# A trunk block on one core: sixteen column blocks of the input projection summed by chunks, and retention moved into the blocks behind them

## The chip, the cores and the metric

The kernel runs on one core of a Trainium2 chip. The metric is the device time of one launch in microseconds (us); the lower, the better. A core has TensorE (PE in the profile; it multiplies matrices and writes PSUM), VectorE (DVE), ScalarE (ACT), GpSimd (POOL) and SyncE (SP, which issues most of the DMAs here). Each engine works through its own list of instructions, and semaphores make it wait for the others.

## The reference, cut to what matters

One layer of a decoder trunk, 256 tokens of 2048 features, all in float32:

```python
mod = silu(c) @ w_ada + b_ada                       # sh1, sc1, g1, sh2, sc2, g2: 2048 each
xn = rmsnorm(h, norm1_g) * (1 + sc1) + sh1
proj = xn @ w_in                                    # 2048 x 18432
q, k, v, g_ret, bg, cg, xc, gate_logits = split(proj)   # 2048 each, gate_logits 4096
q, k = rotary(q, positions), rotary(k, positions)   # 8 heads of 256
y_ret = (norm(retention(q, k, v)) * silu(g_ret)) @ w_ret_o
y_conv = (bg * causal_conv3(cg * xc)) @ w_conv_o
gate_a, gate_b = split(sigmoid(gate_logits + b_gate))
h = h + g1 * ((gate_a * y_ret + gate_b * y_conv) @ w_mix_o)
xn2 = rmsnorm(h, norm2_g) * (1 + sc2) + sh2
h = h + g2 * ((silu(causal_conv3(xn2 @ w_gate) + b) * (xn2 @ w_up)) @ w_down)
out = rmsnorm(h, final_g)
```

## The kernel before

Every weight passes through the core once, as **units** of 256 rows by 512 columns (512 KB). A unit is loaded on SP's queue into one of six `raw` buffers, then prepared: ACT rounds it to a 12-bit `hi` (line 300, `hi<-raw`), DVE takes the rest as `lo` (line 301, `lo<-raw,hi`). PE then multiplies hi by hi, hi by lo and lo by hi, and adds them in PSUM. `hi` and `lo` have three buffers each; in the first stage every third unit lies in a spare buffer of a pool named `big` instead (`hl`).

There are three ways to multiply a unit. `x_block` and `start_block` hold the tokens still and stream the weights: 12 matmuls of 512 columns (lines 372 to 374). `w_block` holds the weights still: 8 matmuls of 512 columns and 8 of 256 (lines 406 and 410). `start_turned` holds the weights still too, with 24 matmuls of 256 columns (lines 517 to 519), so that four tiles of 256 columns fit into two PSUM banks.

The whole program is one list of units, and small calls between them. `w_ada` goes another way: an `Ada` entry is 512 KB that DVE multiplies by a column of silu(c) and adds up (line 337); it has no matmul until its column sums are taken (line 351).

In the first stage xn is not yet known as a whole, since sh1 and sc1 come out of `w_ada`. So it is made in five chunks of its 2048 features (256, 512, 512, 512, 256). After a chunk, the rows of `w_in` which it frees are multiplied for ten column blocks: four of v, four of the swish gate (`sg`), one of q, one of k. The Ada entries of the next chunk are spread between those units by `spread`. A block's sum over a chunk waits in SBUF: ACT copies it out for the first chunk (lines 462 and 523), DVE adds it for each later one (lines 465 and 525), two instructions a block. One gate block keeps its sum in PSUM. Then follow the six other blocks of q and k as `rot_block` (a `w_block`), and behind each pair of them the retention of two heads: DVE turns q and k by the rotary angles (`rotate`, lines 626 to 629), PE makes the scores (653, 656), DVE multiplies them by the decay (660, 661), PE multiplies by v (672 to 674), ACT sums squares (228), POOL takes the root (222), DVE multiplies by that and by the gate (683), PE turns the result (699), and ACT and DVE split it (92, 93). `after(n, f)` puts such a step n entries later. Then come the merge gates and `w_ret_o`, the conv branch (`conv_blocks`, four times three `w_block`s), `w_conv_o`, `w_mix_o` and the feed-forward half, which the change leaves alone.

The loop at the end walks the list: it loads nine entries ahead and prepares four ahead in the first stage, two later. The tile framework then fixes the order on each engine; it goes by this program order, by when buffers come free and by its own estimates.

## Time and profile before

| | |
|---|---|
| median of 3 runs | 1928.77 us (1926.56 to 1931.59) |
| span of the profiled execution | 1927.2 us |
| busy: PE, DVE, ACT, POOL | 1879.1, 1367.4, 904.8, 22.3 us |
| DMA | 450.88 MB, 234 GB/s over the span |
| chain that ended last | PE 92%, DVE 3%, DMA 2% |

The span runs from the first to the last instruction of the profiled execution; no other time of that execution is given, and its span is 1.6 us under the median of the runs. The busy time of matmuls is modelled and overlaps from one to the next, so a PE that is busy all through a stretch has no gap in it, but how fast it goes is read from how many matmuls stand in the stretch.

### The profile page before, as it was taken

What the parts mean: (1) busy time and instruction counts of PE and PEld (TensorE: products, weight loads), DVE (VectorE), ACT (ScalarE), POOL (GpSimd) and SP (SyncE); (2) the same over time, 40 slices, a digit from 0 to 9 for tenths busy, and PEclk for the clock granted to TensorE, in tenths of its full rate; (3) what the DMA queues carried; (4) which work ended last, traced back from release to release, by engine and by line L of the source; (5) the groups of instructions that cost most, each with busy time, mean ns of one, the idle gap of its engine ahead of it and who ended that gap; (6) DMA issues with size and microseconds to landing.
All of it is one profiled execution on the core that took longest, in us unless ns stands there. A gap on an engine that the chain in (4) does not pass through costs nothing.

```text
span 1927.2 us, 26558 instructions
## 1 busy us (share of the span) xinstructions
PE 1879.1 (98%) x10151; PEld 1615.0 (84%) x10151; DVE 1367.4 (71%) x1690; ACT 904.8 (47%) x1187; POOL 22.3 (1%) x52
## 2 busy tenths in 40 slices
PE   5999999999999999999999999999999999999998
PEld 4788888888888888888888787888888888888886
DVE  6889987776766778767777786666665556666655
ACT  3544444444444444444444445555554335555543
POOL 1000000000000000000000000000000000000000
PEclk8899999999999999999999999999999999999999
DMA  8989866666888888787888895666666666666663
GB/s 300 322 305 335 294 217 188 192 201 213 266 266 259 271 263 265 256 279 251 269 270 295 302 321 153 192 186 186 196 189 193 195 190 188 186 188 186 211 192 126
DMA packets 220288, 450.88 MB, mean 234 GB/s; under 512 B 14516, under 2 KB 23040, under 8 KB 219648
## 3 DMA queue, kind: packets, MB, share of 16 engines
q1 hardware_dynamic: 218784, 445.84, 72.4%
q10 hardware_dynamic: 864, 3.15, 0.4%
q8 instruction: 79, 1.29, 0.3%
q14 instruction: 49, 0.40, 0.1%
q0 software_dynamic: 512, 0.20, 0.0%
HBM read 447.03 MB, written 2.10 MB: 233 GB/s over the span
## 4 chain that ended last, share of the span: by engine, by line
PE 92%; DVE 3%; DMA 2%; issue 1%; ACT 1%; POOL 0%; SPq 0%; POOLq 0%; DVEq 0%; ACTq 0%
PE acc L406 41%; PE acc L410 21%; PE acc L373 8%; PE acc L374 8%; PE acc L372 8%; DMA raw<-in_w_ada 2%; DVE lo L301 1%; PE misc L351 1%; PE acc L519 1%; PE acc L517 1%; PE acc L518 1%; DVE ada L337 0%; PE misc L247 0%; PE misc L653 0%; ACT hi L300 0%
## 5 line engine op out<-in xcount | busy, mean ns | idle before, releaser
L406 PE MATMUL acc<-xn,hi 128*128 128x512 f32 x3072 | 1078.6, 396 | 4.5 <-DVE sb L766 2.1
L300 ACT CAST hi<-raw 128x1024 fp32r<-128x1024 f32 x616 | 648.1, 1052 | 845.9 <-PE acc L406 546.6
L301 DVE TENSOR_TENSOR lo<-raw,hi 128x1024 fp32r<-128x1024 f32 x616 | 749.9, 1223 | 361.7 <-ACT hi L300 360.5
L410 PE MATMUL acc<-xn,lo 128*128 128x256 f32 x3072 | 859.8, 280 | 0.0
L406 PEld LDWEIGHTS acc<-xn,hi 128*128 128x128 f32 x3072 | 576.6, 188 | 140.7 <-DVE sb L766 2.4
L410 PEld LDWEIGHTS acc<-xn,lo 128*128 128x128 f32 x3072 | 580.4, 189 | 1.0 <-issue 0.5
L337 DVE SCALAR_TENSOR_TENSOR ada<-raw,c_act,ada 128x1024 f32<-128x1024 f32 (+1 forms) x199 | 239.4, 1203 | 127.2 <-DMA raw<-in_w_ada 126.1
L373 PE MATMUL acc<-lo,ff_t 128*128 128x512 f32 x332 | 129.2, 389 | 0.0
L374 PE MATMUL acc<-hi,ff_t 128*128 128x512 f32 x332 | 129.2, 389 | 0.0
L372 PE MATMUL acc<-hi,ff_t 128*128 128x512 f32 x332 | 129.2, 389 | 0.0
L416 ACT COPY sb<-acc 128x256 f32<-128x256 f32 x224 | 82.3, 367 | 37.9 <-PE acc L410 30.7
L406 PE MATMUL acc<-conv_t,hi 128*128 128x512 f32 x256 | 90.6, 399 | 0.0
L406 PE MATMUL acc<-y_t,hi 128*128 128x512 f32 x256 | 90.2, 396 | 0.0
L410 PE MATMUL acc<-y_t,lo 128*128 128x256 f32 x256 | 72.2, 282 | 1.7 <-DVE lo L301 1.4
L372 PEld LDWEIGHTS acc<-hi,ff_t 128*128 128x128 f32 x332 | 62.3, 188 | 13.1
L374 PEld LDWEIGHTS acc<-hi,ff_t 128*128 128x128 f32 x332 | 62.3, 188 | 13.0
L373 PEld LDWEIGHTS acc<-lo,ff_t 128*128 128x128 f32 x332 | 62.3, 188 | 12.6
L410 PE MATMUL acc<-conv_t,lo 128*128 128x256 f32 x256 | 71.9, 281 | 0.0
L373 PE MATMUL acc<-lo,xn 128*128 128x512 f32 x172 | 69.1, 402 | 1.8 <-DVE lo L301 1.8
L372 PE MATMUL acc<-hi,xn 128*128 128x512 f32 x172 | 68.2, 404 | 1.6 <-ACT hi L300 1.6
L374 PE MATMUL acc<-hi,xn 128*128 128x512 f32 x172 | 68.7, 399 | 0.0
L406 PEld LDWEIGHTS acc<-conv_t,hi 128*128 128x128 f32 x256 | 48.1, 188 | 12.1
(204 smaller groups left out, 1638.2 us busy)
## 6 DMA issues: line engine op xcount, KB each, us to landing
raw<-in_w_in SPq DMA_DIRECT2D x288, 512.0 KB, 4.8
raw<-in_w_ada SPq DMA_DIRECT2D x176, 512.0 KB, 4.6
raw<-in_w_gate SPq DMA_DIRECT2D x88, 512.0 KB, 4.4
raw<-in_w_up SPq DMA_DIRECT2D x88, 512.0 KB, 4.3
raw<-in_w_down SPq DMA_DIRECT2D x88, 512.0 KB, 4.3
raw<-in_w_ret_o SPq DMA_DIRECT2D x32, 512.0 KB, 4.7
raw<-in_w_conv_o SPq DMA_DIRECT2D x32, 512.0 KB, 5.4
raw<-in_w_mix_o SPq DMA_DIRECT2D x32, 512.0 KB, 5.9
```

What stands on the lines that cost most here:

```text
L300: nc.scalar.copy(self.hi, self.raw)
L301: nc.vector.tensor_tensor(self.lo, self.raw, self.hi.bitcast(F32), op=ALU.subtract)
L337: nc.vector.scalar_tensor_tensor(acc, self.raw[:, k], c_act[:, kt:kt + 1], acc, op0=ALU.mult, op1=ALU.add)
L351: nc.tensor.matmul(ps[:, i:i + 1], lhsT=flat[:, (s0 + i) * P:(s0 + i + 1) * P], rhs=ones[:, 0:1], start=True, stop=True,)
L372: nc.tensor.matmul(ps, lhsT=xh, rhs=u.hi[:, k, :], start=k0 + k == first, stop=False)
L373: nc.tensor.matmul(ps, lhsT=xh, rhs=u.lo[:, k, :], start=False, stop=False)
L374: nc.tensor.matmul(ps, lhsT=xl, rhs=u.hi[:, k, :], start=False, stop=k0 + k == end - 1)
L406: nc.tensor.matmul(ps, lhsT=u.hi[:, k, i * P:(i + 1) * P], rhs=xk.rearrange("p h s -> p (h s)"), start=first, stop=False,)
L410: nc.tensor.matmul(ps[:, 0:S], lhsT=u.lo[:, k, i * P:(i + 1) * P], rhs=xk[:, 0, :], start=False, stop=last,)
L416: nc.scalar.copy(b, ps[:, S:2 * S])
L517: nc.tensor.matmul(ps, lhsT=wh, rhs=xk[:, 0, :], start=first, stop=False)
L518: nc.tensor.matmul(ps, lhsT=wh, rhs=xk[:, 1, :], start=False, stop=False)
```

## The change

Sixteen blocks are summed by chunks where ten were: all four blocks of q and of k now go through `start_turned`, in the order v, sg, q, k for each pair of heads. The sums of q and k lie in the pool `big` (the `hl` buffers are gone from it). `rot_block` is gone. The retention of a pair begins (`begin`: both rotations, then the gate's swish) at fixed places in a list made of the last chunk and of the first conv blocks, which moved ahead of the merge gates. All entries are prepared two ahead. `rotate` works in place with one buffer fewer.

```diff
-PREP_START = 4
-TAILS = (0, 6, 3, 4, 6)
+TAILS = (0, 3, 4, 4, 6)
-IN_BIG = (1, 3)
-ROT_AT = 24
-DEFER_SG, DEFER_ROT = (6, 14, 30, 44), 4
+PAIR_AT, PAIR_STEP = 8, 9
-ADA_QK, ADA_RET, ADA_CONV, ADA_OUT = 8, 28, 42, 32
+ADA_LAST, ADA_CONV0, ADA_RET, ADA_CONV, ADA_OUT = 8, 10, 30, 36, 30
...
-                after(DEFER_SG[j - 4], lambda: swish(d))
+                swishes[j - 4].append(lambda: swish(d))
...
-                if k0 + UK == KT:
-                    after(DEFER_ROT, lambda: done(st["sum"]))
...
-    blocks = [start_block(j, j in IN_PSUM) for j in range(8)]
-    ret0 = {}
-    for key in "qk":
-        col = 0 if key == "q" else D
-        blocks.append(start_turned(col, (lambda key: lambda x: rotate(x, ret0, key))(key)))
+    blocks = []
+    for pair in range(4):
+        blocks += [start_block(j, j in IN_PSUM) for j in (pair, 4 + pair)]
+        blocks += [start_turned(i * D + pair * CB, sums_of(pair, i)) for i in range(2)]
...
-        t1 = w4("rot", [P, 4, S])
         o = w4("rotated", [P, 4, S])
-        nc.vector.tensor_tensor(t1, xx, wide(cos_t, 4), op=ALU.mult)
+        nc.vector.tensor_tensor(o, xx, wide(cos_t, 4), op=ALU.mult)
         nc.vector.tensor_tensor(xx, xx, wide(sin_t, 4), op=ALU.mult)
-        nc.vector.tensor_tensor(o[:, 0::2, :], t1[:, 0::2, :], xx[:, 1::2, :], op=ALU.subtract)
-        nc.vector.tensor_tensor(o[:, 1::2, :], t1[:, 1::2, :], xx[:, 0::2, :], op=ALU.add)
+        nc.vector.tensor_tensor(o[:, 0::2, :], o[:, 0::2, :], xx[:, 1::2, :], op=ALU.subtract)
+        nc.vector.tensor_tensor(o[:, 1::2, :], o[:, 1::2, :], xx[:, 0::2, :], op=ALU.add)
...
+        def begin():
+            rotate(qk_sums[pair][:, 0], st, "q")
+            rotate(qk_sums[pair][:, 1], st, "k")
+            for f in swishes[pair]:
+                f()
+            after(3, scores)
...
+    seq = spread(last_chunk, take(ada_mid, ADA_LAST)) + spread(conv_blocks(0), take(ada_mid, ADA_CONV0))
+    for pair in range(4):
+        seq.insert(PAIR_AT + PAIR_STEP * pair, Call(retention(pair)))
+    seq.insert(2, Call(load_decay))
+    units += seq
...
-        ahead = PREP_START if i < n_start else PREP_AHEAD
-        while prepped <= min(i + ahead, n - 1):
+        while prepped <= min(i + PREP_AHEAD, n - 1):
```

Below, the units of the first chunk are called Z0, Z1, ..., those of the last chunk L0 to L15 (v, sg, q, k of pair 0, then of pair 1, and so on), and those of the first conv blocks C0 to C23. So L4 to L7 are v, sg, q and k of pair 1.

First place, the list of DVE where the rotation of pair 0 stands. Before, the eight instructions of the two rotations stand between `lo`s:

```order
L626 TENSOR_TENSOR rot_2452<-sum_565,cos_t 128x1024
L525 TENSOR_TENSOR sum_597<-acc_2370,sum_597 128x512
L525 TENSOR_TENSOR sum_597<-acc_2371,sum_597 128x512
L301 TENSOR_TENSOR lo_2427<-raw_2246,hi_2426 128x1024
L627 TENSOR_TENSOR sum_565<-sum_565,sin_t 128x1024
L337 SCALAR_TENSOR_TENSOR ada_2202<-raw_2367,c_act,ada_2202 128x1024
L301 TENSOR_TENSOR lo_2433<-raw_2268,hi_2432 128x1024
L628 TENSOR_TENSOR rotated_2453<-rot_2452,sum_565 128x2x256
L629 TENSOR_TENSOR rotated_2453<-rot_2452,sum_565 128x2x256
L301 TENSOR_TENSOR lo_2461<-raw_2290,hi_2460 128x1024
L626 TENSOR_TENSOR rot_2480<-sum_597,cos_t 128x1024
```

In the changed kernel the same place reads as follows; `lo_3680` is the `lo` of L6, `acc_3658` the second half of the sum of L4, `acc_3696` and `acc_3697` that of L5, and `lo_3715` the `lo` of L7:

```order
L298 TENSOR_TENSOR lo_3680<-raw_3557,hi_3679 128x1024
L462 TENSOR_TENSOR v_tok_227<-acc_3658,v_tok_227 128x512
L625 TENSOR_TENSOR rotated_3683<-qk_371,cos_t 128x1024
L625 TENSOR_TENSOR rotated_3688<-qk_371,cos_t 128x1024
L626 TENSOR_TENSOR qk_371<-qk_371,sin_t 128x1024 x2
L627 TENSOR_TENSOR rotated_3683<-rotated_3683,qk_371 128x2x256
L628 TENSOR_TENSOR rotated_3683<-rotated_3683,qk_371 128x2x256
L627 TENSOR_TENSOR rotated_3688<-rotated_3688,qk_371 128x2x256
L628 TENSOR_TENSOR rotated_3688<-rotated_3688,qk_371 128x2x256
L462 TENSOR_TENSOR sg_tok_228<-acc_3696,sg_tok_228 128x512
L462 TENSOR_TENSOR sg_tok_229<-acc_3697,sg_tok_229 128x512
L298 TENSOR_TENSOR lo_3715<-raw_3584,hi_3714 128x1024
```

Both rotations now stand in one piece, with no `lo` between the one of L6 and the one of L7.

Second place, the list of DVE where pair 2 begins, behind C0 (whose `lo` is `lo_4100`; the two adds of L15, `qk_767<-acc_4103` and its other half, and the first split `y_t_4131<-misc_4132` stand between that and these rows). Before, such steps of retention had `lo`s between them, as for the second pair:

```order
L301 TENSOR_TENSOR lo_2668<-raw_2458,hi_2667 128x1024
L626 TENSOR_TENSOR rot_2653<-qk_2630,cos_t 128x1024
L301 TENSOR_TENSOR lo_2709<-raw_2486,hi_2708 128x1024
L627 TENSOR_TENSOR qk_2630<-qk_2630,sin_t 128x1024
L93 TENSOR_TENSOR y_t_2691<-misc_2692,y_t_2691 128x2x256
L628 TENSOR_TENSOR rotated_2654<-rot_2653,qk_2630 128x2x256
L629 TENSOR_TENSOR rotated_2654<-rot_2653,qk_2630 128x2x256
L93 TENSOR_TENSOR y_t_2691<-misc_2699,y_t_2691 128x2x256
L301 TENSOR_TENSOR lo_2731<-raw_2508,hi_2730 128x1024
```

And now, up to `lo_4166`, the `lo` of C1:

```order
L90 TENSOR_TENSOR y_t_4131<-misc_4139,y_t_4131 128x2x256
L334 SCALAR_TENSOR_TENSOR ada_3347<-raw_3942,c_act,ada_3347 128x1024
L625 TENSOR_TENSOR rotated_4147<-qk_625,cos_t 128x1024
L625 TENSOR_TENSOR rotated_4152<-qk_625,cos_t 128x1024
L626 TENSOR_TENSOR qk_625<-qk_625,sin_t 128x1024 x2
L627 TENSOR_TENSOR rotated_4147<-rotated_4147,qk_625 128x2x256
L628 TENSOR_TENSOR rotated_4147<-rotated_4147,qk_625 128x2x256
L627 TENSOR_TENSOR rotated_4152<-rotated_4152,qk_625 128x2x256
L628 TENSOR_TENSOR rotated_4152<-rotated_4152,qk_625 128x2x256
L477 TENSOR_TENSOR sg_tok_228<-sg_tok_228,sig_4157 128x512
L477 TENSOR_TENSOR sg_tok_229<-sg_tok_229,sig_4160 128x512
L298 TENSOR_TENSOR lo_4166<-raw_3973,hi_4165 128x1024
```

Fifteen instructions, those of a split, an Ada step, two rotations and the swish among them, now stand between the `lo` of C0 and that of C1. For pair 1 ten stand between those of L11 and L12, for pair 3 ten between those of C6 and C7.

Third place, the list of ACT in the first chunk. Before, the first units are all of v, and the copies of one (line 462) stand ahead of the next `hi`:

```order
L300 CAST hi_334<-raw_299 128x1024
L462 COPY v_tok_227<-acc_317 128x512
L462 COPY v_tok_226<-acc_350 128x512
L462 COPY v_tok_227<-acc_351 128x512
L300 CAST hi_368<-raw_332 128x1024
L462 COPY v_tok_226<-acc_384 128x512
L462 COPY v_tok_227<-acc_385 128x512
L300 CAST hl_402<-raw_366 128x1024
```

In the changed kernel `hi_403` belongs to Z4 and `hi_459` to Z5; `acc_369` is a sum of Z2, `acc_407` and `acc_408` those of Z3, `acc_441` and `acc_442` those of Z4:

```order
L297 CAST hi_342<-raw_283 128x1024
L297 CAST hi_365<-raw_303 128x1024
L520 COPY qk_371<-acc_369 128x512
L520 COPY qk_371<-acc_370 128x512
L297 CAST hi_403<-raw_312 128x1024
L520 COPY qk_371<-acc_407 128x512
L520 COPY qk_371<-acc_408 128x512
L459 COPY v_tok_226<-acc_441 128x512
L459 COPY v_tok_227<-acc_442 128x512
L297 CAST hi_459<-raw_340 128x1024
L297 CAST hi_468<-raw_363 128x1024
```

So the `hi` of Z5 stands behind copies of the very unit ahead of it, Z4; the same holds for Z9, behind copies of Z8. From Z4 on, the `hi`s of the other units stand behind copies of the unit two ahead, or of none; that of Z14 also has the six instructions ahead of it that make xn of the second chunk.

## Rows read from the trace of the kernel before

**Rows 1.** The page: busy time, and the span in 40 equal slices.
```profile
PE 1879.1 (98%) x10151; PEld 1615.0 (84%) x10151; DVE 1367.4 (71%) x1690; ACT 904.8 (47%) x1187; POOL 22.3 (1%) x52
...
PE   5999999999999999999999999999999999999998
...
DVE  6889987776766778767777786666665556666655
...
PEclk8899999999999999999999999999999999999999
```

**Rows 2.** Windows by stage: stretch, length, each engine's busy us (instructions), granted clock, DMA.
```profile
32.68:70.26 37.58, 29.44 (x91) 20.47 (x92) 31.70 (x33) 17.06 (x24) 0.00 (x0) 0.71 0.90 308
70.26:97.80 27.54, 27.54 (x145) 23.77 (x144) 22.19 (x22) 13.86 (x18) 0.00 (x0) 1.00 0.95 321
97.80:280.12 182.32, 181.68 (x977) 157.41 (x976) 167.61 (x212) 80.17 (x89) 0.00 (x0) 1.00 0.87 293
280.12:460.00 179.88, 179.48 (x1031) 157.02 (x1030) 134.82 (x172) 78.59 (x121) 4.05 (x4) 1.00 0.63 193
460.00:480.00 20.00, 18.78 (x106) 15.90 (x105) 11.46 (x13) 9.37 (x15) 0.00 (x0) 1.00 0.66 217
```

**Rows 3.** Windows: 13 units of 512-column matmuls, 4 of `start_turned`, 7 of `w_block`.
```profile
143.84:179.20 35.36, 35.36 (x157) 29.28 (x156) 35.36 (x37) 11.63 (x12) 0.00 (x0) 1.00 1.00 357
126.82:138.34 11.52, 11.52 (x98) 11.52 (x96) 9.51 (x13) 7.97 (x11) 0.00 (x0) 1.00 0.72 223
317.56:336.97 19.41, 19.41 (x114) 16.98 (x113) 13.76 (x15) 8.66 (x11) 0.00 (x0) 1.00 0.68 217
```

**Rows 4.** Groups of DVE by form: count | busy us, mean ns | idle before.
```profile
L301 DVE TENSOR_TENSOR lo<-raw,hi 128x1024 fp32r<-128x1024 f32 x616 | 749.9, 1223 | 361.7 <-ACT hi L300 360.5
L337 DVE SCALAR_TENSOR_TENSOR ada<-raw,c_act,ada 128x1024 f32<-128x1024 f32 x169 | 217.0, 1284 | 126.9 <-DMA raw<-in_w_ada 126.1
L465 DVE TENSOR_TENSOR v_tok<-acc,v_tok 128x512 f32<-128x512 f32 x32 | 21.4, 686 | 1.6 <-PE acc L374 1.4
L626 DVE TENSOR_TENSOR rot<-qk,cos_t 128x1024 f32<-128x1024 f32 x6 | 7.3, 1224 | 0.1
L628 DVE TENSOR_TENSOR rotated<-rot,qk 128x512 f32<-128x512 f32 x6 | 4.1, 688 | 0.1
L660 DVE TENSOR_TENSOR pt<-misc,decay 128x256 f32<-128x256 f32 x8 | 3.4, 420 | 0.6 <-PE misc L656 0.6
L661 DVE TENSOR_TENSOR pt<-misc,decay 128x128 f32<-128x128 f32 x8 | 2.3, 282 | 0.0
L683 DVE SCALAR_TENSOR_TENSOR y_tok<-misc,r_y,sg_tok 128x256 f32<-128x256 f32 x16 | 6.6, 478 | 4.7 <-POOL r_y L222 4.7
L93 DVE TENSOR_TENSOR y_t<-misc,y_t 128x512 fp32r<-128x512 f32 x8 | 5.2, 683 | 0.0
```

**Rows 5.** Chain that ended last, retention of pair 0: start us, us, what.
```profile
294.42 0.86 PE misc L653 x4
...
296.59 0.44 PE misc L656 x4
...
302.59 0.43 PE misc L672 x2
...
304.75 0.45 PE misc L674 x2
...
311.30 0.87 PE misc L699 x8
```

**Rows 6.** Timeline of the first chunk: start us, us, engine, instruction [idle before <-releaser].
```profile
42.96 0.59 ACT L462 COPY v_tok<-acc 128x512 f32<-128x512 f32 x1 [0.54 <-PE acc L374]
43.44 1.05 ACT L300 CAST hi<-raw 128x1024 fp32r<-128x1024 f32 x1
44.54 0.73 PE L372 MATMUL acc<-hi,xn 128*128 128x512 f32 x2 [1.62 <-ACT hi L300]
...
46.46 0.50 PE L373 MATMUL acc<-lo,xn 128*128 128x512 f32 x1 [1.18 <-DVE lo L301]
```

More of the change, by code (lines that the diff above doesn't have):

```diff
@@ L496, in start_block, with start_turned @@
                 for n, ch in enumerate(chunks)]
-    def start_turned(col, done):
+    def start_turned(col, sums):
         st = {}
@@ L507, in run @@
                 if k0 == 0:
-                    st["sum"] = w4("sum", [P, 4, S])
+                    st["sum"] = sums()
                 for i in range(4):
@@ L531, in start_turned, with sums_of, sums @@
                 for n, ch in enumerate(chunks)]
-    blocks = [start_block(j, j in IN_PSUM) for j in range(8)]
-    ret0 = {}
-    for key in "qk":
-        col = 0 if key == "q" else D
-        blocks.append(start_turned(col, (lambda key: lambda x: rotate(x, ret0, key))(key)))
+    qk_sums = {}
+    swishes = [[] for _ in range(4)]
+    def sums_of(pair, i):
+        def sums():
+            if pair not in qk_sums:
+                qk_sums[pair] = blk8("qk", [P, 2, 4, S], F32)
+            return qk_sums[pair][:, i]
+        return sums
+    blocks = []
+    for pair in range(4):
+        blocks += [start_block(j, j in IN_PSUM) for j in (pair, 4 + pair)]
+        blocks += [start_turned(i * D + pair * CB, sums_of(pair, i)) for i in range(2)]
     def spread(seq, extra, tail=0):
@@ L556, in tile_trunk_block @@
         seq = [u for b in blocks for u in b[n]]
-    units += seq
-    for i, u in enumerate([u for u in units if isinstance(u, Weights)]):
-        u.in_big = i % IN_BIG[1] < IN_BIG[0]
     units.insert(40, Call(turn_vectors))
     units.insert(5, Call(prep=lambda: turned(*vec1)))
-    units.insert(len(units) - ROT_AT, Call(rest_of_rotary))
-    units.insert(len(units) - ROT_AT + 6, Call(sines))
-    n_start = len(units) - 12
+    units.insert(len(units) - 10, Call(rest_of_rotary))
+    units.insert(len(units) - 4, Call(sines))
+    last_chunk = seq
     g1b = {}
@@ L703, in turn @@
                 split(ps.rearrange("p (k s) -> p k s", k=2), yb[:, 2 * g:2 * g + 2])
-        st["next"] = scores
-        return st
+        def begin():
[4 more added lines that the diff above has]
+            after(3, scores)
+        return begin
     def load_decay():
@@ L710, in load_decay @@
         tc.keep_in_program_order(nc.scalar.dma_start(dec["t"], decay))
-    units.insert(len(units) - 8, Call(load_decay))
-    seq = []
-    for pair in range(4):
-        st = retention(pair, ret0 if pair == 0 else {})
-        if pair > 0:
-            seq += rot_block(pair * CB, st, "q")
-            seq += rot_block(D + pair * CB, st, "k")
-    units += spread(seq, take(ada_mid, ADA_QK))
     def gate_block(col, store, key):
@@ L730, in gate_block @@
         return in_block(col, e)
-    mixp = {}
-    def ret_block(j, store):
-        def e(i, a, b):
-            if j % 2 == 0 and i == 0:
-                mixp[j // 2] = blk8("mixp", [P, 8, S], F32)
-            nc.vector.tensor_tensor(b, a, b, op=ALU.add)
-            nc.vector.tensor_tensor(
-                mixp[j // 2][:, (4 * j + i) % 8, :], b, store["g"][:, i, :], op=ALU.mult
-            )
-        return w_block(w_ret_o, j * CB, lambda kt: y_t[kt // 4][:, kt % 4], e)
-    seq = []
-    for j in range(4):
-        st = {}
-        seq += gate_block(7 * D + j * CB, st, "g")
-        seq += ret_block(j, st)
-    units += spread(seq, take(ada_mid, ADA_RET))
     conv_t = []
@@ L786, in conv_blocks, with ret_block, e @@
                 + in_block(4 * D + j * CB, e_b))
+    seq = spread(last_chunk, take(ada_mid, ADA_LAST)) + spread(conv_blocks(0), take(ada_mid, ADA_CONV0))
[3 more added lines that the diff above has]
+    units += seq
+    mixp = {}
+    def ret_block(j, store):
+        def e(i, a, b):
+            if j % 2 == 0 and i == 0:
+                mixp[j // 2] = blk8("mixp", [P, 8, S], F32)
+            nc.vector.tensor_tensor(b, a, b, op=ALU.add)
+            nc.vector.tensor_tensor(
+                mixp[j // 2][:, (4 * j + i) % 8, :], b, store["g"][:, i, :], op=ALU.mult
+            )
+        return w_block(w_ret_o, j * CB, lambda kt: y_t[kt // 4][:, kt % 4], e)
     seq = []
     for j in range(4):
+        st = {}
+        seq += gate_block(7 * D + j * CB, st, "g")
+        seq += ret_block(j, st)
+    units += spread(seq, take(ada_mid, ADA_RET))
+    seq = []
+    for j in range(1, 4):
         seq += conv_blocks(j)
```

14 lines of the change are left out of this document (2 added, 12 removed).

## The prediction

> **What bounds the kernel now.** I read the page first, then windows by stage, then one window for each kind of unit, then the groups of DVE, and last the chain and the timeline where a term needs them. The page shows PE busy 98% and DVE 71% [rows 1]; the 40 slices show that this share of DVE is an average over first slices with digits of 8 and 9 and a rest with 5 to 7. The windows say where PE is not busy. From 32.68 to 70.26 us it has 29.44 busy us of 37.58, at a mean granted clock of 0.71 (between the two levels, 1.2 and 2.4 GHz); from there to 460 us it lacks 1.0 us in 390 in all [rows 2]. So PE's work sets the time; what a change can win ahead of 460 us lies in the first chunk, and whatever keeps PE waiting later is added in full.
>
> PE does a unit in 35.36 / 13 = 2.72 us with 512-column matmuls, 11.52 / 4 = 2.88 us in `start_turned`, and 19.41 / 7 = 2.77 us in `w_block` [rows 3]. In the first chunk it did six units in 37.58 us, where 6 x 2.72 = 16.3 would do: 21.3 us are lost there.
>
> DVE was busy 167.61 of 182.32 us from 97.80 on, without making PE wait [rows 2]: a DVE that is 92% busy isn't yet the bound. What matters is how many units stand prepared when a long piece of DVE work comes.
>
> **The change, part by part.**
>
> *Kind of unit.* Six blocks of eight units go from `w_block` to `start_turned`: 48 x (2.88 - 2.77) = +5.3 us on PE. The rows show both kinds at full clock and without a gap, so I give this no range of its own. The Trainium skill ("TensorE: Matmul & The Clock Gate", section "Wait — 56ns, not 53.3ns?") gives a warm matmul N / 2.4 GHz + 2.5 ns from start to start. By that estimate the two kinds would take 2.62 and 2.60 us, and this term would be 1 us; the row is 10% slower for the turned kind and 6% for the other, so it decides.
>
> *Chunks 2 to 4.* They have 96 units where they had 60, half of them turned, so PE needs 5.6 us for two. DVE in these 5.6 us has two `lo`s (2.45), the sums of one block (1.37) and at most 1.14 Ada steps (1.46) [rows 4]: 5.3 us. Before, 0.94 Ada steps came with one unit, and DVE had more to do a unit than now. The first adds of a block wait for PE, but two units are prepared by then, 5.6 us of cover. I cost this at nothing; if Ada loads are late, DVE's slack of 0.3 us per two units is gone, and it costs up to 8 us (0.08 a unit), which I keep for the range. More adds by chunks on DVE (the 48 units bring 6 x 4 x 2 of them) are in these sums.
>
> *First chunk.* Sixteen units instead of ten, with one or two Ada steps behind a unit, not four. What PE waits for there is seen in the timeline: the copy of a unit, the `hi` behind it on ACT, PE idle 1.62 us, then 1.18 us for the `lo` [rows 6], 2.8 us in all. That wait is not an Ada wait; it comes from ACT's order, and the changed order keeps it for Z5 and Z9 (third place shown): 5.6 us. Z0 and Z1 keep their 11.9 us (from 32.68 [rows 2] to the third unit at 44.54), where 5.4 would do: 6.4 lost. The six instructions of xn ahead of Z14's `hi` are 3.6 us at most (0.6 each, as the copy in the same rows). The clock was at half for part of this stretch (mean 0.71); for two such waits I allow two units at half clock, each 2.7 us longer, +5.4. Sum 21.0 against 21.3: **0 us**. Bounds: -13 if only the loads bind (a rival, below), +8 if the half clock stays (three more such units).
>
> *Retention moved.* This is the large term. Before, one `lo` or more stood within each rotation. Now each pair's two rotations stand in one piece: 4 x 1.22 + 4 x 0.69 = 7.6 us [rows 4], and the next `lo` behind them. PE can use only units whose `lo` stands ahead of the piece.
> - Pair 0: PE ends L4; DVE then has half a sum (0.69), rotations 7.6, the sum of L5 (1.37), `lo` of L7 (1.22): 10.9 us. PE has L5 and L6, 5.6. Gap 5.3.
> - Pair 1: after the `lo` of L11 rotations, swish (1.37) and `lo` of L12: 10.2; PE has L11, 2.9. Gap 7.3.
> - Pair 2: after the `lo` of C0 the sum of L15 (1.37), split (1.37), Ada (1.28), rotations, swish, `lo` of C1: 14.2; PE has C0, 2.8. Gap 11.5.
> - Pair 3: after the `lo` of C6 split, rotations, `lo` of C7: 10.2; PE has C6, and about one unit more, since DVE has caught up by then: 10.2 - 5.5. Gap 4.7.
>
> Together 28.8 us. The scores of each pair fall into these gaps: 294.42 to 297.03, 2.6 us that PE spends beside no wait today [rows 5], so 4 x 2.6 = 10.4 come off: 18.4. Between the gaps DVE stays late. From the `lo` of L7 to that of L11 it has four `lo`s (4.9), five sums (6.9), two Ada steps (2.6), the decay products (1.4), `y_tok` (1.9) and a split (1.4): 19.1 us [rows 4], while PE has 11.2 us of units, 2.6 of mixing by v (302.59 to 305.20) and 0.9 of turning [rows 5]: +4.4. From L12 to C0 the same count without the split and with one sum less is 16.3 against 14.7: +1.6. From C1 to C6 PE has more (17.4 against 14.6). So 24.4. DVE also waits in its own list for the root and for the squares (4.7 us for four pairs for the root [rows 4]); when DVE is the bound this counts, with PE's part at half clock after a gap I put it at 4.6. Term **+29 us**. Bounds: 18 (gaps less scores alone) and 45 (four gaps, each followed by two units at half clock, +5.4 each, less what later gaps hide).
>
> *Rest.* From 460 to 480 us PE lacks 1.2 us, where `w_ret_o` begins right behind the last pair [rows 2]; now 24 conv units lie between: -1.2 us. The conv blocks only change place, the Ada entries move by a few; SP's queue has the same 512 KB loads, and the DMA share in this stretch was 0.63 [rows 2]. Buffers in `big` are enough, as the `hl`s make room for the sums of q and k. Nothing for these.
>
> Sum: 1927.2 + 5.3 + 0 + 29 - 1.2 = 1960.3 us by the span of the profiled execution; the median of the runs is 1.6 us above that span, so **1962 us**, 1.7% slower.
>
> **The rivals.**
> - *Half clock in the gaps.* A clock of 0.71 over the first chunk came with waits of 1 to 3 us [rows 2, 6]; the gaps here are 5 to 11. If PE falls to half each time and DVE waits for its slow units, each pair costs 4 us more: 1978 us. Against it: most of these slow units lie beside DVE work. The Trainium skill (the same page, section "HAM oscillation — how this bites in real kernels") tells of a kernel that falls back to half clock after every wait for a load; the 0.71 agrees with that, and it speaks for this rival.
> - *The first chunk is won back.* Sixteen units take 65.1 us now (32.68 to 97.80). Each comes with 2.23 loads of 512 KB, 3.8 us at the 308 GB/s of that stretch [rows 2], 3.3 at the 357 of a later one [rows 3]. If ACT's order costs little and the loads run at 357, sixteen units take 52.3 us: 13 come off, 1949 us, slower still.
> - *Preparation never holds PE (the other side).* If units stood prepared three ahead at each piece, as PE's full windows from 70 us on suggest of the kernel before, the 29 us are gone, and so are the waits of the first chunk: 1927.2 + 5.3 - 13 - 1.2 + 1.6 = 1920 us, faster. From the point where the gaps come to under 15 us with the first chunk at its best, the kernel isn't measurably slower. Against it: `hi` and `lo` have three buffers each and the list of DVE is fixed; only where DVE is far ahead could a piece be covered, and its adds tie it to PE.
>
> **How the numbers follow.** The forecast 0.56, half clock 0.18, the first chunk won back 0.15, preparation covered in full or in part 0.11. A time within 0.3% (5.8 us) can't be told from no change here. The last rival gives 0.07 faster and, where it holds in part, 0.04 within that bound; all else, 0.89, is slower. The range leaves out that rival and the far end of the half clock: 1940 to 1987 us.
>
> **What would show it.** By PE's units the last chunk begins near 97.8 + 96 x 2.8 = 367 us, some more with the column sums. From about 385 to 480 us DVE should be busy at 95% or more, with four idle pieces of PE of 5 to 11 us, each ended by a `lo` (line 298) behind line 628 or 477. The turned units should take 2.88 us, and the seventeenth unit should start near 98 us, as before. Wrong would be: PE full through 385 to 480 us (then the order doesn't bind as I read it), PE waiting in chunks 2 to 4 for a `lo` behind an Ada step, or a seventeenth unit before 85 or after 106 us.

## The result, and the profile after

The changed kernel takes 1963.69 us (median of four runs, 1959.89 to 1965.57), the kernel before 1928.37 us on the same chip: ratio 1.0172, 95% interval 1.0149 to 1.0194. The forecast was 1962 us. The profiled execution has a span of 1961.8 us, 34.6 more than before.

The page of the changed kernel, with the same lines as [rows 1] (busy time, 40 slices of 49 us):

```profile
PE 1890.0 (96%) x10535; PEld 1636.9 (83%) x10535; DVE 1385.2 (71%) x1714; ACT 904.9 (46%) x1175; POOL 24.1 (1%) x52
...
PE   5999999988999999999999999999999999999998
...
DVE  6788778899776667787677676766665556666655
...
PEclk9999999989999999999999999999999999999999
```

The shares of the whole span hardly differ. The slices tell the place: the two from 392 to 490 us have an 8 on PE, the first of them a lower clock too, and they are the two in which DVE shows a 9. Windows by stage, as [rows 2] (length, busy us of PE, PEld, DVE, ACT, POOL, then granted clock, DMA share, GB/s). The stages are the first 16 units; the 96 units of chunks 2 to 4; four turned units among them; the last chunk with conv 0 (40 units, and the retention); the gates and `w_ret_o`; `w_conv_o`:

```profile
31.08:90.27 59.19, 52.74 (x308) 45.18 (x308) 43.00 (x43) 35.83 (x52) 0.00 (x0) 0.94 0.86 292
90.27:368.66 278.39, 275.42 (x1770) 250.84 (x1769) 224.39 (x267) 111.28 (x115) 0.00 (x0) 1.00 0.80 261
101.18:112.69 11.51, 11.51 (x98) 11.51 (x96) 8.83 (x10) 4.20 (x4) 0.00 (x0) 1.00 0.92 308
368.66:533.82 165.16, 149.19 (x835) 130.89 (x834) 143.20 (x197) 64.99 (x104) 5.86 (x5) 0.93 0.58 191
533.82:721.18 187.36, 183.87 (x1059) 159.43 (x1058) 128.74 (x147) 84.95 (x113) 1.66 (x3) 1.00 0.80 265
927.15:1119.12 191.97, 185.77 (x1031) 158.72 (x1029) 135.22 (x157) 89.14 (x118) 1.44 (x2) 0.99 0.79 263
```

Where the 34.6 us are, by the first matmul of each stage in both traces:

| Part | Forecast | Measured | How |
|---|---|---|---|
| kind of unit | +5.3 | +5.3 | 11.51 / 4 = 2.88 us a turned unit, as forecast; 48 x 0.11 |
| start and first 16 units | 0 | -8.5 | first unit 1.6 earlier, 59.19 against 65.12 us; 1.0 of turned units taken off |
| chunks 2 to 4 | 0 | +3.6 | 9.6 us over 96 x 2.8; before, 64 units (50 x 2.72 + 14 x 2.88) had 6.0 over theirs |
| retention | +29 | +29.1 | 165.16 + 187.36 us are 63.9 over 16 x 2.8 + 88 x 2.77; before, the 112 units from 280.12 to 625.15 us were 34.8 over theirs |
| rest | -1.2 | +5.1 | conv -1.6, `w_conv_o` +7.6 (191.97 against 184.34), the stages behind it -0.9 |

So the large term came out, and two terms costed at nothing did not, with opposite signs.

The retention stretch was limited from DVE's side, as forecast, but it looks otherwise than forecast. What PE waits for in 368.66 to 533.82 us (us in total, times, longest), and then what DVE waits for:

```profile
PE misc L640 <- DVE rotated L627: 9.5, 3, 6.3
PE acc L516 <- DVE lo L298: 5.1, 2, 3.3
```

```profile
DVE ada L334 <- DMA raw<-in_w_ada: 7.0, 3, 5.3
DVE y_tok L670 <- POOL r_y L219: 4.2, 4, 1.2
DVE lo L298 <- ACT hi L297: 4.2, 6, 1.5
```

PE is idle for 165.16 - 149.19 = 16.0 us, not four times 5 to 11, and most of it ends with the scores (L640), which stand ahead of the next unit's lo products in PE's list. The rest of the loss is in the clock. Two windows around pair 2:

```profile
440.00:450.00 10.00, 6.87 (x45) 5.74 (x44) 10.00 (x15) 3.18 (x5) 0.00 (x0) 1.00 0.50 153
450.00:460.00 10.00, 6.35 (x24) 5.41 (x25) 10.00 (x14) 1.78 (x3) 0.00 (x0) 0.66 0.22 71
```

DVE has no idle moment in these 20 us. Its timeline there shows the piece that the prediction wrote out for pair 2 (sum, split, Ada, two rotations, swish, then `lo`), row for row; a bracket with the idle time before an instruction stands nowhere:

```profile
442.36 1.21 DVE L298 TENSOR_TENSOR lo<-raw,hi 128x1024 fp32r<-128x1024 f32 x1
443.49 1.28 DVE L522 TENSOR_TENSOR qk<-acc,qk 128x512 f32<-128x512 f32 x2
444.69 1.27 DVE L90 TENSOR_TENSOR y_t<-misc,y_t 128x512 fp32r<-128x512 f32 x2
445.88 1.27 DVE L334 SCALAR_TENSOR_TENSOR ada<-raw,c_act,ada 128x1024 f32<-128x1024 f32 x1
447.08 2.35 DVE L625 TENSOR_TENSOR rotated<-qk,cos_t 128x1024 f32<-128x1024 f32 x2
449.35 2.35 DVE L626 TENSOR_TENSOR qk<-qk,sin_t 128x1024 f32<-128x1024 f32 x2
...
454.03 1.28 DVE L477 TENSOR_TENSOR sg_tok<-sg_tok,sig 128x512 f32<-128x512 f32 x2
455.23 2.35 DVE L298 TENSOR_TENSOR lo<-raw,hi 128x1024 fp32r<-128x1024 f32 x2
```

PE's timeline at the same place, the scores behind their wait:

```profile
453.65 2.05 PE L640 MATMUL misc<-rotated,rotated 128*128 128x256 f32 x4 [6.28 <-DVE rotated L627]
```

One wait was not foreseen at all: at the start of the stretch DVE stands still for an Ada load, behind the 1 MB load of the decay table, and PE then for 3.3 us (DVE's timeline):

```profile
378.23 1.28 DVE L334 SCALAR_TENSOR_TENSOR ada<-raw,c_act,ada 128x1024 f32<-128x1024 f32 x1 [5.31 <-DMA raw<-in_w_ada]
```

### The profile page after: what moved, and what is told of

It reads as the page before. It is cut to its first block, busy times and chain, and to the rows that moved or that the text cites. A ratio compares the mean times of both kernels' runs of the same rounds, so it can differ in the third digit from the quotient of the medians.

```text
span 1961.8 us, 27384 instructions
## 1 busy us (share of the span) xinstructions
PE 1890.0 (96%) x10535; PEld 1636.9 (83%) x10535; DVE 1385.2 (71%) x1714; ACT 904.9 (46%) x1175; POOL 24.1 (1%) x52
## 4 chain that ended last, share of the span: by engine, by line
PE 80%; DMA 9%; DVE 7%; issue 2%; ACT 1%; POOL 0%; SPq 0%; DVEq 0%; POOLq 0%; ACTq 0%
PE acc L403 35%; PE acc L407 18%; DMA raw<-in_w_ada 9%; PE acc L370 7%; PE acc L371 7%; PE acc L369 7%; DVE lo L298 3%; PE acc L516 2%; PE acc L514 2%; PE acc L515 2%; DVE ada L334 1%; PE misc L348 1%; PE misc L640 1%; ACT hi L297 0%; PE misc L244 0%
## 5 line engine op out<-in xcount | busy, mean ns | idle before, releaser
L297 ACT CAST hi<-raw 128x1024 fp32r<-128x1024 f32 x643 | 675.8, 1052 | 894.4 <-PE acc L403 474.9
L298 DVE TENSOR_TENSOR lo<-raw,hi 128x1024 fp32r<-128x1024 f32 x643 | 779.8, 1221 | 327.1 <-ACT hi L297 325.5
L403 PE MATMUL acc<-xn,hi 128*128 128x512 f32 x2688 | 944.0, 397 | 8.3 <-DVE sb L786 3.2
L407 PE MATMUL acc<-xn,lo 128*128 128x256 f32 x2688 | 749.8, 279 | 0.6 <-DVE lo L298 0.5
L403 PEld LDWEIGHTS acc<-xn,hi 128*128 128x128 f32 x2688 | 505.2, 188 | 129.9 <-DVE sb L786 3.8
L407 PEld LDWEIGHTS acc<-xn,lo 128*128 128x128 f32 x2688 | 507.4, 189 | 2.5 <-DVE lo L298 1.4
L516 PE MATMUL acc<-xn,lo 128*128 128x256 f32 x512 | 146.4, 289 | 7.8 <-DVE lo L298 7.8
L514 PE MATMUL acc<-xn,hi 128*128 128x256 f32 x512 | 146.8, 287 | 0.8 <-ACT hi L297 0.8
L515 PE MATMUL acc<-xn,hi 128*128 128x256 f32 x512 | 146.4, 287 | 0.0
L516 PEld LDWEIGHTS acc<-xn,lo 128*128 128x128 f32 x512 | 99.7, 196 | 9.4 <-DVE lo L298 9.4
L369 PE MATMUL acc<-hi,xn 128*128 128x512 f32 x256 | 100.7, 399 | 6.6 <-ACT hi L297 3.5
L370 PE MATMUL acc<-lo,xn 128*128 128x512 f32 x256 | 102.2, 399 | 2.4 <-DVE lo L298 2.4
L514 PEld LDWEIGHTS acc<-xn,hi 128*128 128x128 f32 x512 | 100.2, 196 | 1.9 <-ACT hi L297 1.1
L371 PE MATMUL acc<-hi,xn 128*128 128x512 f32 x256 | 101.3, 396 | 0.0
L515 PEld LDWEIGHTS acc<-xn,hi 128*128 128x128 f32 x512 | 100.2, 196 | 0.8
L413 ACT COPY sb<-acc 128x256 f32<-128x256 f32 x200 | 73.6, 368 | 44.0 <-PE acc L407 31.4
```

The source lines that it names most:

```text
L297: nc.scalar.copy(self.hi, self.raw)
L298: nc.vector.tensor_tensor(self.lo, self.raw, self.hi.bitcast(F32), op=ALU.subtract)
L369: nc.tensor.matmul(ps, lhsT=xh, rhs=u.hi[:, k, :], start=k0 + k == first, stop=False)
L370: nc.tensor.matmul(ps, lhsT=xh, rhs=u.lo[:, k, :], start=False, stop=False)
L371: nc.tensor.matmul(ps, lhsT=xl, rhs=u.hi[:, k, :], start=False, stop=k0 + k == end - 1)
L403: nc.tensor.matmul(ps, lhsT=u.hi[:, k, i * P:(i + 1) * P], rhs=xk.rearrange("p h s -> p (h s)"), start=first, stop=False,)
```

## The experiments

Each edit is made to the changed kernel unless it says otherwise. Over all profiled executions the feed-forward half, which no edit touches, took from 741.4 to 748.0 us, with PE idle for 9.3 us in each; chunks 2 to 4 took 275.2 to 280.3 us where no edit touches them. So single executions differ by some us for reasons of no edit, and the verdicts rest on the stage that an edit touches. "The three stages" are last chunk, conv 0 and gates with `w_ret_o`: 352.5 us in the changed kernel. In experiments 3, 4 and 11, which leave these stages alone, they took 347.8, 352.7 and 350.4 us; last chunk and conv 0 by themselves took 165.2 to 166.0 us in the four kernels, the gate stage 182.2 to 187.4. By the same sum that gave 63.9 above, a retention that costs no more than before would come to some 323 us (352.5 - 29).

**1. The rotations cut.** `begin` did both rotations at once. Now `rotate` keeps the two products, a new `rotate2` has the difference and the sum, and `begin` spreads the four pieces:

```diff
-            rotate(qk_sums[pair][:, 0], st, "q")
-            rotate(qk_sums[pair][:, 1], st, "k")
-            for f in swishes[pair]:
-                f()
-            after(3, scores)
+            q, k = qk_sums[pair][:, 0], qk_sums[pair][:, 1]
+            rotate(q, st, "q")
+            after(1, lambda: rotate2(q, st, "q"))
+            after(2, lambda: rotate(k, st, "k"))
+            after(3, lambda: rotate2(k, st, "k"))
+            after(4, lambda: [f() for f in swishes[pair]])
+            after(5, scores)
```

> The rotations of a pair are cut into four pieces that begin one entry after another, with a lo between them, the swish one entry later and the scores two entries later; nothing is left out. Theory A (the undivided piece: PE runs out of prepared units while DVE works through 7.6 us without a lo): last chunk, conv 0 and the gate and ret_o stage fall from 73.98, 91.17 and 187.36 us to about 53, 75 and 182, and the time from 1964 to some 1930 to 1942 us. Theory B (the rate: in 368.66 to 533.82 us DVE has 143.2 us of work where PE needs about 136, so it stays busy whatever the order): PE still waits for DVE, only in more and shorter pieces; at most 10 us come back, time 1954 us or more.

Measured: 1957.26 us (1952.80 to 1961.27), ratio to before 1.0156 (1.0124 to 1.0187), not to be told from the changed kernel's. The three stages take 347.2 us, 5.3 less. The window of last chunk and conv 0:

```profile
365.76:527.62 161.86, 144.77 (x834) 125.52 (x833) 142.89 (x197) 65.31 (x104) 6.30 (x5) 0.98 0.61 195
```

The window is 3.3 us shorter; the rest of the 5.3 is within what the gate stage differs by without an edit. Theory A falls: without the long piece PE is idle as long as with it (17.1 us against 16.0). Its clock came back (0.98 instead of 0.93, 4.4 us of its busy time), and what the window is shorter is DVE's idle time, 19.0 us (161.86 - 142.89) instead of 22.0.

**2. Ada steps out of the stretch.**

```diff
-ADA_LAST, ADA_CONV0, ADA_RET, ADA_CONV, ADA_OUT = 8, 10, 30, 36, 30
+ADA_LAST, ADA_CONV0, ADA_RET, ADA_CONV, ADA_OUT = 0, 0, 38, 44, 32
```

> The 18 Ada steps that stand in the last chunk and conv 0 are moved behind them (0, 0, 38, 44, 32 instead of 8, 10, 30, 36, 30; 12 instead of 14 are left for later stages); the rotations stay in one piece. Theory B (rate): DVE has 18 x 1.28 = 23 us less to do in the stretch, and the 8.8 us that it waited there for Ada loads go too, so some 20 us come back: 1940 to 1946 us. Theory A (undivided piece): only the 1.28 us that stand inside one piece and part of the lateness between the gaps come back, 1955 to 1962 us. Against both: 38 and 44 steps in the next stages may make PE wait there, seen as longer gate and conv stages than 187.36 and 205.98 us.

Measured: 1948.73 us (1946.33 to 1954.16), ratio 1.0122 (1.0086 to 1.0157). The three stages take 333.4 us, 19.1 less, as theory B has it; conv 1 to 3, with 44 steps beside 72 units, grow from 205.98 to 212.48 us. But this edit does two things: pairs are placed by entries, so with fewer entries they also stand further apart. Experiments 9 and 10 try to separate these. And it does a third: the tile framework divided the rotations of pairs 2 and 3 by itself here (pair 2 into one, five and two instructions), so that only pairs 0 and 1 have whole pieces.

```profile
367.02:516.03 149.01, 139.03 (x818) 122.93 (x817) 125.10 (x181) 64.25 (x103) 4.10 (x5) 0.99 0.51 158
```

**3. The first chunk's Ada steps dense.**

```diff
-TAILS = (0, 3, 4, 4, 6)
+TAILS = (0, 12, 4, 4, 6)
```

> The 16 Ada steps of the second chunk are spread over the first 4 of the 16 units of the first chunk, as densely as in the kernel before (16 over 4), where the changed kernel spreads them over 13. Theory C (the 8.5 us that the first chunk gained come from this spreading, which keeps the loads of units and Ada steps flowing side by side): the first chunk goes from 59.2 to 65 us or more, time about 1970 to 1974 us. Rival D (the gain comes from the order of the blocks, two of them turned, or from the order of ACT): first chunk stays within 2 us of 59.2, time 1962 to 1966 us.

Measured: 1970.49 us (1965.07 to 1973.83); the first 16 units take 65.7 us, 6.5 more, as theory C has it. The `hi`s of Z2 and Z3 wait 3.6 and 1.1 us there for their loads, and ACT's order is another one too. Experiment 7 shows that this is half of the story.

**4. One Ada step behind every second unit of `w_conv_o`** (`ADA_CONV, ADA_OUT` 34, 32 instead of 36, 30).

> Two Ada steps move from conv 1 to 3 to the conv_o stage: 34 and 32 instead of 36 and 30, so that the 64 units of conv_o have exactly one step behind every second unit, as in the kernel before. Theory E (the 7.6 us that conv_o became longer come from the uneven spacing of 30 steps over 64 units, behind which DVE waits in its list for a late Ada load): conv_o falls from 191.96 to about 184.3 us, time 1955 to 1958 us. Rival F (another cause, such as the loads themselves being slower or later there): conv_o stays within 2 us of 192, time 1962 to 1966 us.

Measured: 1958.60 us (1953.93 to 1966.88); the stage takes 188.5 us, between the two theories. Over all runs it took 188.7 to 193.6 us with 30 steps (seven kernels, mean 190.8), 183.0 to 188.6 with 32 (five, mean 186.9), and 184.3 and 185.2 in the kernel before and experiment 7. So some 4 us go with the number of steps, though other edits differ between these kernels too; 2 stay unexplained, and the 7.6 us of the one profile are partly chance. DVE waits for Ada loads 49.1 us in this stage in the changed kernel and 41.6 here; PE is idle 6.2 us there and 5.2 here, and not at all in the kernel before.

**5. The decay table loaded earlier.**

```diff
-    seq.insert(2, Call(load_decay))
+    units.insert(len(units) - 30, Call(lambda: load_decay()))
```

> The 1 MB load of the decay table is issued some 30 entries earlier, in the fourth chunk, instead of at the third entry of the last chunk. In the trace of the changed kernel DVE waits 5.31 us there for an Ada load issued 1.3 us behind it, and PE stands idle 3.45 us at 377 us. Theory G (the shared DMA engines make this Ada load late, and DVE, which is full until 480 us, never makes it good): the wait goes and the last chunk gets 4 to 6 us shorter, time 1956 to 1960 us. Rival H (the same load delays another Ada step, or the wait has another cause): PE waits as long in the fourth chunk, time 1962 to 1966 us.

Measured: 1963.29 us (1962.14 to 1968.81). The last chunk is 5.0 us shorter (69.0), and chunks 2 to 4 are 3.2 longer: rival H. The wait went along with the load. DVE's timeline, and PE's:

```profile
298.16 0.68 DVE L522 TENSOR_TENSOR qk<-acc,qk 128x512 f32<-128x512 f32 x1
304.61 0.75 DVE L334 SCALAR_TENSOR_TENSOR ada<-raw,c_act,ada 128x512 f32<-128x512 f32 x1 [5.76 <-DMA raw<-in_w_ada]
```

```profile
307.81 0.79 PE L370 MATMUL acc<-lo,xn 128*128 128x512 f32 x1 [3.21 <-DVE lo L298]
```

The decay load was issued at 295.95 us on ACT's queue, the Ada loads at 296.25 on SP's. The Trainium skill ("DMA: Bandwidth & Descriptors", section "Issuing engines are not separate DMA queues") says that DMAs of different issuing engines run on the same 16 DMA engines; an Ada load that is late behind a load of another queue agrees with that.

**6. The rotations on GpSimd** (`nc.gpsimd` for `nc.vector` in the four instructions of `rotate`).

> The four instructions of each rotation go to GpSimd, idle there but for the roots; everything else stays. Theory B (the rate of DVE): DVE's 143 us of work in the last chunk, conv 0 and the start of the gate stage fall by 8 x 3.8 = 30 us, under PE's need; 18 to 29 us come back, time 1935 to 1946 us. Theory A, by now weak, says about the same, since the piece leaves DVE's list. Rival I (GpSimd is so slow, or slows DVE so much while both run, that the scores wait for it): time 1960 us or more, with PE waiting for rotated from POOL.

Measured: 1985.23 us (1981.94 to 1988.61), ratio 1.0293 (1.0249 to 1.0336): rival I. What PE waits for from 367 to 555 us, then groups of POOL and of DVE by form from 385 to 485 us:

```profile
PE misc L640 <- POOL rotated L627: 26.1, 4, 8.3
```

```profile
L625 POOL TENSOR_TENSOR rotated<-qk,cos_t 128x1024 f32<-128x1024 f32 x7 | 18.6, 2675 | 0.0
L627 POOL TENSOR_TENSOR rotated<-rotated,qk 128x512 f32<-128x512 f32 x6 | 13.3, 2210 | 0.2
```

```profile
L298 DVE TENSOR_TENSOR lo<-raw,hi 128x1024 fp32r<-128x1024 f32 x18 | 36.5, 2025 | 0.8 <-ACT hi L297 0.8
L334 DVE SCALAR_TENSOR_TENSOR ada<-raw,c_act,ada 128x1024 f32<-128x1024 f32 x9 | 15.0, 1664 | 0.0
L522 DVE TENSOR_TENSOR qk<-acc,qk 128x512 f32<-128x512 f32 x12 | 7.8, 680 | 0.0
```

A product that took DVE 1.22 us takes POOL 2.7 to 3.1, and `lo` goes from 1.22 to 2.03 us meanwhile. So this run relieves DVE of less than it seems, and is no test of theory B.

**7. The kernel before, its first Ada steps spread** (`TAILS = (0, 2, 3, 4, 6)` instead of `(0, 6, 3, 4, 6)`).

> The kernel before with one number changed: the 16 Ada steps of its second chunk stand over the first 8 of its 10 units instead of the first 4. Theory C (dense Ada steps hold back the loads of the units, so PE and the loads take turns): the first 16 units fall from 65.1 us by 3 to 8 us, time 1919 to 1924 us against 1926 for the kernel before on this chip. Rival J (with ten units the loads alone bind, or the gain needs the two turned units between): no change, within 2 us of the kernel before.

Measured: 1929.81 us (1925.58 to 1936.60, ten runs) against 1925.12, ratio 1.0017 (0.9996 to 1.0037); its first 16 units take 65.9 us, where they took 65.1. Rival J: spreading alone gives the kernel before nothing.

**8. Ada steps out, rotations cut, decay early** (0, 0, 38, 36, 32, with the edits of 1 and 5).

> Three edits of the changed kernel together: no Ada steps in the last chunk and conv 0 (0, 0, 38, 36, 32; 22 left for the stage of w_mix_o instead of 14), the rotations cut into pieces as in the first experiment, and the decay table loaded early. By theory B (rate) with the runs so far: 1949 with the Ada steps out, 6 less since conv 1 to 3 keep their 36 steps, up to 8 more of the 10 us that PE still lost in the stretch there: 1934 to 1943 us, slower than the kernel before still. If cutting is worth as little as it was alone, 1941 to 1946. If 22 steps in the stage of w_mix_o are too many, that stage is longer than 101 us by up to 10.

Measured: 1937.01 us (1929.46 to 1949.48, ten runs), ratio 1.0053 (1.0029 to 1.0077): the fastest of the new order, and still slower than the kernel before. The three stages take 328.6 us, and PE has a clock of 1.00 there:

```profile
370.81:510.73 139.92, 136.34 (x811) 120.85 (x810) 123.11 (x175) 63.32 (x102) 4.10 (x5) 1.00 0.54 162
```

Conv 1 to 3 have 204.2 us again, and the 22 steps in the stage of `w_mix_o` cost nothing there (100.3 us). So some 24 of the 29 us come from the stretch; a part of them is the wait for the late Ada load, which lies in the fourth chunk here, as in experiment 5.

**9. Ada steps out, the pairs where they were.** As experiment 2, with `PLACES = (5, 12, 18, 24)` for the pairs.

> As the second experiment (0, 0, 38, 44, 32), which also moved the pairs apart, since they are placed by entries and the Ada steps are entries; here each pair begins behind the same unit as in the changed kernel (L4, L10, L15, C4). Theory B (rate: 23 us less of DVE work beside the retention is what gave the gain): last chunk, conv 0 and gate stage together stay near the 333.4 us of the second experiment, where the changed kernel has 352.5; time 1944 to 1952 us. Theory K (the distance of the pairs: six units between two of them are too few for DVE to catch up): the sum is 343 us or more, time 1953 to 1962 us.

**10. Ada steps kept, the pairs apart.** `PLACES = (12, 25, 37, 50)`.

> The Ada steps stay where the changed kernel has them (8, 10, 30, 36, 30), and the pairs begin behind the units at which the second experiment had them (L7, L15, C7, C15), eight units apart instead of five or six. Theory B (rate): DVE's work in the stretch is the same 143 us, so at most some 8 us come back, from the end of the stretch, where DVE has slack: sum of the three stages 344 us or more, time 1954 to 1962 us. Theory K (distance): most of the 19 us of the second experiment come back: sum 333 to 340 us, time 1943 to 1951 us.

Measured: 9 takes 1956.53 us (1951.34 to 1958.41), the three stages 343.5; its rotations stand behind the `lo`s of L6, L12, C2 and C7, those of the changed kernel behind L6, L11, C0 and C6. 10 takes 1964.61 us (1962.31 to 1968.79), the three stages 357.8. The windows of 9 and of 10:

```profile
365.52:522.93 157.41, 145.51 (x819) 127.70 (x817) 126.10 (x181) 64.43 (x104) 4.10 (x5) 0.95 0.50 147
```

```profile
366.28:534.78 168.50, 148.21 (x835) 130.44 (x833) 142.59 (x195) 64.62 (x104) 5.38 (x5) 0.94 0.59 190
```

Neither theory stands as it was put. Distance beside the Ada steps makes it 5.3 us worse, so K falls; here too the framework divided rotations, those of pairs 0, 2 and 3. With 17 us less of DVE work at nearly the same places only 9.0 us come back, less than half of what B asked. What is left in 9 are four gaps of 2.4 to 4.2 us, each at a whole rotation piece, in front of the scores or of the `lo` behind it: the thing that theory A spoke of. Hence the next theory (N): DVE needs slack over the stretch, and no piece may be longer than what stands prepared; each alone helps little.

**11. Half the Ada bytes beside the first chunk.**

```diff
-                nc.sync.dma_start(self.raw[:, k], self.cols(w_ada[r0:r0 + P, :]))
+                n = self.width // 2 if self.half else self.width
+                nc.sync.dma_start(self.raw[:, k, :, 0:n], self.cols(w_ada[r0:r0 + P, :])[:, :, 0:n])
...
+            u.half = n == 1
```

> The 16 Ada steps beside the first chunk load half of their bytes: 256 of 512 columns of each run, and DVE adds these to both halves in two instructions of half the size, so that its work stays (half of the second chunk's shifts and scales are thus taken from other columns). The first 16 units then come with 24 instead of 32 times 512 KB. Theory L (the loads set the first chunk: 17.3 MB in 59.2 us in the changed kernel, 20.4 MB in 65.1 us in the one before, both near 300 GB/s): about 4 MB less, the 16 units take 48 to 52 us, time 1952 to 1957 us. Theory M (ACT's order: copy, hi and lo one behind another at Z5 and Z9, and the late xn): 57 to 60 us, time 1961 to 1965 us.

Measured: 1952.02 us (1948.13 to 1959.89). The first 16 units take 50.1 us, within theory L's 48 to 52, and PE waits 0.2 us in them:

```profile
31.68:81.77 50.09, 49.87 (x307) 44.74 (x307) 42.42 (x55) 34.41 (x52) 0.00 (x0) 0.95 0.85 278
```

But the edit changed more than the bytes. The tile framework, which goes by its own estimates, also laid ACT's list out anew. In the changed kernel both copies of Z4 (`v_tok`) stand ahead of the `hi` of Z5 (ACT's timeline):

```profile
47.18 0.59 ACT L459 COPY v_tok<-acc 128x512 f32<-128x512 f32 x1 [1.03 <-PE acc L371]
48.31 0.59 ACT L459 COPY v_tok<-acc 128x512 f32<-128x512 f32 x1 [0.54 <-PE acc L371]
48.80 1.99 ACT L297 CAST hi<-raw 128x1024 fp32r<-128x1024 f32 x2
```

Here the `hi` of Z5 stands ahead of both, and that of Z6 between them:

```profile
45.37 1.05 ACT L297 CAST hi<-raw 128x1024 fp32r<-128x1024 f32 x1 [0.48 <-DMA raw<-in_w_in]
46.33 0.58 ACT L531 COPY qk<-acc 128x512 f32<-128x512 f32 x1
47.13 0.59 ACT L470 COPY v_tok<-acc 128x512 f32<-128x512 f32 x1 [0.23 <-PE acc L382]
48.92 1.05 ACT L297 CAST hi<-raw 128x1024 fp32r<-128x1024 f32 x1 [1.19 <-DMA raw<-in_w_in]
49.87 0.58 ACT L470 COPY v_tok<-acc 128x512 f32<-128x512 f32 x1
```

The `hi` of Z9 likewise stands ahead of the copies of Z8. So the run has the time of theory L and doesn't decide between L and M. For the waits at Z5 and Z9 the traces speak for M: in the first 16 units of the changed kernel ACT waits for no load, while here nine `hi`s do, 6.3 us in all, and PE hardly waits.

**12. Ada steps out at the same places, and the rotations cut** (9 with the edit of 1).

> The Ada steps are out of the stretch (0, 0, 38, 44, 32) and the pairs stand behind L4, L10, L15 and C4, as in the run before the last two, and the rotations are cut into pieces as in the first run. There PE lost four gaps of 2.4 to 4.2 us with DVE full for 10 us around each. Theory N (two conditions at once: DVE must have slack over the stretch, and no piece may be longer than what stands prepared; either one alone gives little): most of these 11.9 us go, the three stages come to 330 to 336 us where that run had 343.5 and cutting alone 347.2; time 1942 to 1950 us. Theory K (also the distance between the pairs is needed): the sum stays at 340 us or more, time 1953 us or more.

Measured: 1944.58 us (1941.71 to 1949.06), ratio 1.0083 (1.0058 to 1.0108). The three stages take 331.8 us: theory N.

```profile
365.86:508.47 142.61, 138.66 (x818) 121.47 (x817) 123.04 (x178) 64.63 (x104) 7.29 (x5) 1.00 0.54 161
```

The cases side by side, in us; idle and busy are PE's in last chunk and conv 0:

| Ada steps | Rotations | Pairs | PE idle | PE busy | Clock | Three stages |
|---|---|---|---|---|---|---|
| in | whole | near | 16.0 | 149.2 | 0.93 | 352.5 |
| in | cut | near | 17.1 | 144.8 | 0.98 | 347.2 (-5.3) |
| in | partly divided | apart | 20.3 | 148.2 | 0.94 | 357.8 (+5.3) |
| out | whole | near | 11.9 | 145.5 | 0.95 | 343.5 (-9.0) |
| out | cut | near | 4.0 | 138.7 | 1.00 | 331.8 (-20.7) |
| out | partly divided | apart | 10.0 | 139.0 | 0.99 | 333.4 (-19.1) |

The single edits are worth 5.3 and 9.0 us, where kernels alike in these stages differ by up to 4.9, and together 20.7. By last chunk and conv 0 alone (idle and busy added) they are worth 3.3, 7.8 and 22.5 us, where such kernels differ by 0.8. The last row says one thing more: with the Ada steps out, pairs further apart come to 333.4 us as well, though pairs 0 and 1 have whole pieces there. So once DVE has slack, more units between the pieces give about what cutting gives; distance with whole pieces only was not run.

## Why the forecast was right, step by step

**Kind of unit: right.** 2.88 us, +5.3.

**Retention: right in sum and in the engine named, wrong in its parts.** The prediction summed gaps of PE. Measured are 16.0 us of idle time, 3.3 of them behind the late Ada load that the prediction did not have, and some 9 to 11 us of matmuls at the lower clock (149.2 us busy, 1.8 of them 16 column sums that experiments 12 and 8 have elsewhere, against 138.7 and 136.3 there at clock 1.00). At the pieces of the four pairs PE is idle 1.4, 1.8, 6.3 and 0 us, where the gaps less the scores gave 2.7, 4.7, 8.9 and 2.1. The step that failed is the split between idle and slow. It cost hardly anything in the sum, since DVE set the end: in 368.66 to 533.82 us it has 143.2 us of work and stands idle for 22, and PE, which needs some 137, fills the time by waiting or by going slower. Experiment 1 bears that out in part: 4.4 us of slow time went, 1.1 us of idle time came, and the stretch got shorter by what DVE was idle less. The sum would have been shorter on DVE's side: its work in the stretch, plus its waits in order.

The reason given, "one piece", was half of it. The other half is the rate, which the prediction counted only between the gaps. Experiments 9, 1 and 12 show that with the pairs at these places both must go; by experiment 2, more distance can stand in for the cut.

**First chunk: mis-sized, 0 forecast, -8.5 measured.** Over PE's own need (8 x 2.72 + 8 x 2.88 = 44.8 us) the 16 units lose 14.4 us, where the prediction kept 21.0. ACT's order did what the prediction said: the waits at Z5 and Z9 stand there, 1.62 us for `hi` and 0.53 for `lo` each, 4.3 us against 5.6. At Z5:

```profile
49.90 0.73 PE L369 MATMUL acc<-hi,xn 128*128 128x512 f32 x2 [1.62 <-ACT hi L297]
51.16 0.50 PE L370 MATMUL acc<-lo,xn 128*128 128x512 f32 x1 [0.53 <-DVE lo L298]
```

The column sums and xn at Z12 to Z14 cost 4.3 us, against 3.6 for xn. Mis-sized were Z0 and Z1, which take 8.5 us (31.08 to 39.62), 3.1 lost instead of 6.4, and the slow matmuls, 2.7 us (what remains) instead of 5.4.

The step that failed is "That wait is not an Ada wait", by which the losses of the kernel before were kept whatever the Ada steps do. With four of these behind a unit the first five units take 34.5 us in the kernel before and 34.0 in experiment 3, where `hi` waits for loads; with one or two behind a unit they take 18.8 in the changed kernel. Two things stay open: why spreading gives the kernel before nothing (experiment 7, in which ACT waits 14.7 us for loads), and whether the further 9.1 us of experiment 11 come from fewer bytes or from ACT's other order.

In size the -8.5 us lie towards the rival "first chunk won back", but not by its mechanism: the loads ran at 292 GB/s and not at 357, and ACT's order kept its price. Its 2.23 loads a unit don't come out of the rows either: 37.58 x 308 + 27.54 x 321 = 20.4 MB [rows 2] are 39 loads of 512 KB in 16 units, 2.43 each.

**Chunks 2 to 4: +3.6, within the 8 kept for them.** 2.9 us are idle pieces of PE of up to 0.7 us, each ended by a `lo` and most with an Ada step right ahead of that `lo`. That is the second of the signs of being wrong; it came, at a small price.

**Rest: +5.1 instead of -1.2.** The prediction had "Nothing for these" beside -1.2 us where `w_ret_o` begins; the conv blocks gave -1.6. `w_conv_o` grew: PE is idle 6.2 us in it, about 4 us go with the number of Ada steps, and the others are open.

**The rivals.** The half clock came (0.66 in the second window around pair 2, 0.93 over the stretch), but not with 4 us a pair on top of the 29, for the reason above. The Trainium skill's account of a kernel that falls back after every wait ("TensorE: Matmul & The Clock Gate", section "HAM oscillation — how this bites in real kernels") agrees with the clock at waits of 3.3, 1.8 and 6.3 us: the 10 us from 380, 420 and 450 us have 0.66, 0.62 and 0.66. It doesn't agree at each wait: behind the 1.62 us at Z9 the clock stayed at 1.00 (65.40 to 69.04 us). That preparation never holds PE is refuted by the 16.0 us that PE waits in the stretch. Of "what would show it", the last chunk's start (368.66 against 367 or more) and DVE's share from 385 to 480 us (89.0 of 95, 94%) came near, while the four idle pieces of 5 to 11 us were one of 6.3 and smaller ones, three of them ended by `rotated` and not by a `lo`.

The 1962 us thus owe something to chance: -8.5, +3.6 and +6.3 were not foreseen and nearly cancel.
